# Log-sum-exp over eight heads: two heads transposed on TensorE and summed by matmuls with exp(bias), in place of three heads biased in PSUM

## The chip, the cores and the metric

The kernel runs on one core of one Trainium2 chip. The metric is the device time of one execution in microseconds (us), as the median of several runs. The core has five engines with an instruction stream each: TensorE (PE in the profile), VectorE (DVE), ScalarE (ACT), GpSimd (POOL) and SyncE (SP); here SP issues nearly all of the transfers between device memory and the on-chip SBUF. PSUM is the memory that TensorE writes.

## The reference

```python
B, S, D, H = 8, 2048, 2048, 8          # x: (B, S, D) float32, bias: (H, D // H) float32
Dh = D // H                            # 256
x_heads = x.reshape(B, S, H, Dh).transpose(0, 2, 1, 3) + bias[None, :, None, :]
x_tiled = np.repeat(x_heads, 2, axis=2)
mx = x_tiled.max(axis=-1, keepdims=True)
lse = mx.squeeze(-1) + np.log(np.exp(x_tiled - mx).sum(axis=-1))     # (B, H, 2 * S)
```

For each batch, row and head the kernel needs the logarithm of a sum of 256 exponentials of x + bias, and it writes each result twice. The input x has 134.2 MB and is read once. Both kernels compute the sum without subtracting the maximum, note in a flag whether a sum or a bias lay outside bounds within which that is safe, and branch at the end to a general routine if one did. With this input the routine is not entered.

## The kernel before, in words

**Tiles.** A tile is 256 rows of one batch: 128 partitions, K = 2 rows in each, 2048 columns, 2 MB. There are T = 64 tiles, eight to a batch. SBUF has room for eight (`xts`, which are halves of four 4 MB buffers `xbs`). Up to tile 41 one transfer brings two tiles (4 MB, L175); from `BLOCKS = 42` on one transfer brings one tile (2 MB, L187), and from tile 57 on one row of 1 MB, the last in pieces of columns. A transfer into a buffer waits until the last readers of the tiles that were in it (`last_uses`) are done. It is issued from `reload`, behind the tile after.

**A bulk tile** (tiles 0 to 53, mode `BULK`). The eight heads go three ways:
- Heads 0 to 2: TensorE puts the bias into PSUM with a matmul of a matrix of ones (L289), and adds x with an identity matmul (`late_heads`, L348). ScalarE takes exp of head 0 from PSUM and adds it up itself (L359), one instruction for each of the two rows; of heads 1 and 2 it writes the exp back over x (L366).
- Head 3: ScalarE takes exp of x without the bias, and VectorE multiplies it by exp(bias), which lies in PSUM (`later`, L416).
- Heads 4 to 7: GpSimd adds the bias to x (L398), and ScalarE takes exp (L404, together with head 3).
- VectorE then sums heads 1 to 7 of both rows in one reduction of 3584 elements in each partition (L423).

**The last tiles** have other modes: from tile 54 `MIXED`, from tile 57 row by row. There VectorE weighs a head and sums it in one instruction (`weigh`, L439) followed by one that reads the sum out; GpSimd folds one or two heads (`fold`, L455 and L463); and `keep_warm` issues three matmuls of the identity for each row (L339).

**At the end of a batch**, two tiles late, `finish` does this: VectorE clips the 128 sums of each partition, compares them and adds the result to `bad` (L482, L485, L489); TensorE transposes the sums (L496); and ScalarE takes the logarithm and doubles it (L506). `store` writes seven batches at once (L510), `finish_last` the eighth (L529).

**Order.** The order on each engine is that of the calls (a manual schedule). The two lists `for_pool` and `for_pe` put off some calls until the next tile. Waits between engines follow from the data; a reader that is known to come later than another is declared free of a wait (`on_x`).

Of the kernel before, what the change touches and what calls it, by code (L numbers as in the profile page):

```python
# [10 lines left out]
BF16 = mybir.dt.bfloat16  # L11
ACT = mybir.ActivationFunctionType
ALU = mybir.AluOpType

# [4 lines left out]
BLOCKS = 42  # L19

NBUF = 8

NEARLY = 5

NWARM = 3
# [7 lines left out]
GENERAL_B = 2  # L33

BULK = dict(pe=3, acc=1, g0=4, late=True, fold=0)
MIXED = dict(pe=1, acc=1, g0=4, late=False, fold=0)
PROMPT_F1 = dict(pe=2, acc=2, g0=8, late=False, fold=1)
PROMPT_F2 = dict(pe=2, acc=2, g0=8, late=False, fold=2)
SINGLE_F1 = dict(pe=1, acc=1, g0=8, late=False, fold=1)
TRIPLE = dict(pe=3, acc=3, g0=8, late=False, fold=0)
FOLD = 32

STAGES = [
    (0, (BULK,)),  # L50
    (54, (MIXED,)),
    (57, (PROMPT_F1, PROMPT_F1)),
    (62, (SINGLE_F1, SINGLE_F1)),
    (63, (PROMPT_F2, TRIPLE)),
]

LAST_COLS = [
    [(0, 512), (1280, 2048), (512, 1280)],
    [(0, 512), (768, 1280), (1280, 1792), (512, 768), (1792, 2048)],
]  # L60
# [3 lines left out]
def kernel(  # L64
# [11 lines left out]
    NBLK = S // (P * K)  # L76
    NB = S // (P * KB)
    TB = KB // K
    T = B * NBLK
    T_PROMPT = STAGES[1][0]  # L80
    T_FACTORS = T // 2
    CPE = BULK["pe"] * Dh
    MM = 512


    V0, W0, G0, W1, W2 = Dh, 3 * Dh, 4 * Dh, 6 * Dh, 7 * Dh
# [5 lines left out]

    brow = sb.tile([1, D], F32, name="brow")
    b_rep = sb.tile([P, D - G0], F32, name="b_rep")
    w_sb = sb.tile([P, D - W1], F32, name="w_sb")
    ident = sb.tile([P, P], F32, name="ident")
    ones = sb.tile([1, P], F32, name="ones")
    ones3 = sb.tile([3, P], BF16, name="ones3")
    b3 = sb.tile([3, CPE], BF16, name="b3")
    bparts = sb.tile([1, 3, CPE], BF16, name="bparts")  # L100
    brest = sb.tile([1, 2, CPE], F32, name="brest")
    b_flat = sb.tile([P, D // P], F32, name="b_flat")
    held = sb.tile([P, P], F32, name="held")
    out_of = sb.tile([P, P], F32, name="out_of")
    bad = sb.tile([P, P], F32, name="bad")
    ones_k = sb.tile([P, 1], F32, name="ones_k")
    flag = sb.tile([1, 1], F32, name="flag")
    g_max = sb.tile([P, GB * H], F32, name="g_max")
    g_sum = sb.tile([P, GB * H], F32, name="g_sum")
    g_res = sb.tile([P, GB, H, 2], F32, name="g_res")  # L110

    R = [sb.tile([P, KB, H, NB], F32, name=f"R{b}") for b in range(B - 1)]
    R_last = sb.tile([P, H, NBLK, K], F32, name="R_last")
    res = sb.tile([H * NB, B - 1, P, KB, 2], F32, name="res")
    res_last = sb.tile([P, P, 2], F32, name="res_last")
    xbs = [sb.tile([P, KB, D], F32, name=f"xb{i}") for i in range(NBUF // TB)]
    xts = [xb[:, k : k + K] for xb in xbs for k in range(0, KB, K)]
    w_ps = pp.tile([P, W2 - W0], F32, name="w_ps")


    one_ps = pp.tile([P, MM], F32, name="one_ps")
    pairs = [pp.tile([P, 2 * MM], F32, name=f"pair{i}") for i in range(2)]
    ps = [p[:, c : c + MM] for p in pairs for c in (0, MM)]
    tp = pp.tile([P, KB, P], F32, name="tp")

    def modes_of(t):
        return [modes for t0, modes in STAGES if t0 <= t][-1]

    def pieces(t):

        if len(modes_of(t)) == 1:
            return [(0, K, 0, D)]
        cols = [[(0, D)]] * K if t < T - 1 else LAST_COLS
        return [(k, k + 1, c0, c1) for k in range(K) for c0, c1 in cols[k]]

    def rows_of(t, n=1):


        b, at = divmod(t, NBLK)
        if b < B - 1:  # L140
            blk, i = divmod(at, TB)
            v = x[b, blk * P * KB : (blk + 1) * P * KB, :]
            return v.rearrange("(p k) d -> p k d", k=KB)[:, i * K : (i + n) * K]
        v = x[b, at * P * K : (at + 1) * P * K, :]
        return v.rearrange("(k p) d -> p k d", k=K)

    users = [[] for _ in xbs]

    def on_x(t, ins, after):
        buf = users[t // TB % len(xbs)]
        for t_u, u in buf:
            same = u.ins.engine == ins.ins.engine
            if u not in after and (not same or t_u % NBUF == t % NBUF and t_u < t):
                tc.declare_no_dep(
                    ins.ins,
                    u.ins,
                    reason="another tile, or waited for by those it waits for",
                )  # L160
        buf.append((t, ins))
        return ins

    loads = {}

    last_uses = [[] for _ in range(T)]

    def load(t):
        if TB <= t < BLOCKS:

            if t % TB == 0:
                after = [u for i in range(TB) if t >= NBUF for u in last_uses[t + i - NBUF]]
                ins = on_x(
                    t,
                    nc.sync.dma_start(  # L175
                        out=xbs[t // TB % len(xbs)], in_=rows_of(t, TB)
                    ),
                    after,
                )
                for i in range(TB):  # L180
                    loads[t + i, 0, 0] = ins
            return
        after = last_uses[t - NBUF] if t >= NBUF else []
        for k0, k1, c0, c1 in pieces(t):
            loads[t, k0, c0] = on_x(
                t,
                nc.sync.dma_start(  # L187
                    out=xts[t % NBUF][:, k0:k1, c0:c1],
                    in_=rows_of(t)[:, k0:k1, c0:c1],
                ),  # L190
                after,
            )

    def reload(t):

        n = t + NBUF
        if n < BLOCKS:
            if n % TB == TB - 1:
                load(n - TB + 1)
        elif n < T:  # L200
            load(n)
# [3 lines left out]

# [10 lines left out]
    nc.scalar.dma_start(out=brow, in_=bias.rearrange("h j -> (h j)").unsqueeze(0))  # L216
    for t in range(NBUF):
        load(t)
    nc.scalar.dma_start(
        out=b_flat, in_=bias.rearrange("h j -> (h j)").rearrange("(p c) -> p c", p=P)  # L220
    )
    nc.vector.memset(ones, 1.0)
    nc.vector.memset(ones_k, 1.0)
    nc.vector.memset(bad, 0.0)
    nc.vector.memset(ones3, 1.0)
    make_identity(nc, ident)


    bp = brow[:, 0:CPE]
    nc.gpsimd.tensor_copy(bparts[:, 0], bp)  # L230
    nc.gpsimd.tensor_sub(brest[:, 0], bp, bparts[:, 0])
    nc.gpsimd.tensor_copy(bparts[:, 1], brest[:, 0])
    nc.gpsimd.tensor_sub(brest[:, 1], brest[:, 0], bparts[:, 1])
    nc.gpsimd.tensor_copy(bparts[:, 2], brest[:, 1])
    for i in range(3):
        nc.scalar.dma_start(out=b3[i : i + 1, :], in_=bparts[:, i])

    def spread(dst, c0, c1):  # L240
        nc.tensor.matmul(  # L241
            dst, lhsT=ones, rhs=brow[:, c0:c1], start=True, stop=True
        )

    for i, c in enumerate(range(G0, D, MM)):
        spread(ps[i], c, c + MM)
        nc.vector.tensor_copy(b_rep[:, c - G0 : c - G0 + MM], ps[i])
    w_late = w_ps[:, 0 : G0 - W0]
    spread(w_late, W0, G0)
    nc.scalar.activation(out=w_late, in_=w_late, func=ACT.Exp)  # L250

    def first_factors():
        spread(one_ps, V0, W0)
        nc.scalar.activation(out=one_ps, in_=one_ps, func=ACT.Exp)

    def other_factors():
        nc.scalar.activation(
            out=w_ps[:, G0 - W0 :], in_=b_rep[:, 0 : W2 - G0], func=ACT.Exp
        )
        nc.scalar.activation(out=w_sb, in_=b_rep[:, W1 - G0 :], func=ACT.Exp)  # L260


    n_ps = [0]


    bank_users = [[], []]

    def on_bank(i, ins):
        for j, u in bank_users[i // 2]:
            if j != i and u.ins.engine != ins.ins.engine:  # L270
                tc.declare_no_dep(ins.ins, u.ins, reason="another bank")
        bank_users[i // 2].append((i, ins))
        return ins

    def put_bias(m, k0, k1):
# [3 lines left out]
        if m["late"]:  # L279
            pair = pairs[n_ps[0] % 2]  # L280
            n_ps[0] += 1
            got = [one_ps, pair[:, 0:MM], pair[:, MM : 2 * MM]]

            parts = [(ones3, b3)]
            if n_ps[0] <= NEARLY:
                parts = [(ones3[0:1], bparts[:, i]) for i in range(3)]
            for h, p in enumerate(got):
                for i, (lhsT, b) in enumerate(parts):
                    nc.tensor.matmul(  # L289
                        p,  # L290
                        lhsT=lhsT,
                        rhs=each_row(b, h * Dh, Dh, K),
                        start=i == 0,
                        stop=False,
                    )
# [427 lines left out]
```

## Time and profile before

| | us |
|---|---|
| median of 3 runs | 347.09 (346.72 to 347.30) |
| profiled execution, its time | 347.54 |
| profiled execution, its span | 345.8 |
| busy in the span: DVE / POOL / PE / ACT | 317.2 / 287.7 / 271.0 / 263.5 |
| mean granted TensorE clock | 0.879 of full speed |

The profile is of one execution. Its span reaches from the first to the last instruction; what lies around the span is 347.54 - 345.8 = 1.7 us. Busy time counts each engine's own instructions, and engines run beside one another, so an engine's share says how full it is and not whether it sets the end. For that the profile has the chain of waits: it is followed back from the last instruction, at each step to what released it. The clock row gives the clock that the throttle granted to TensorE, in tenths of full speed. GB/s is what the 16 DMA engines moved.

### The profile page before, as it was taken

The page shows a single profiled execution, that of the slowest core. Times are in us where ns is not written, and L with a number is a line of the kernel's source. Part 1 is how long each engine was busy: PE and PEld are TensorE (multiplying, and loading weights), DVE is VectorE, ACT ScalarE, POOL GpSimd, SP SyncE. Part 2 cuts the span into 40 slices and gives each one's busy share as a digit, 9 for nine tenths or more (in the row PEclk, how much of TensorE's full clock was granted, in tenths as well). Part 3 has the DMA queues.
Part 4 walks back from the last instruction along what each step waited for, and adds up shares of the span by engine and source line. Part 5 has one row for each costly group of instructions (what it writes and reads, how often), then busy time and mean ns, then how long its engine had stood idle before and what let it go on. Part 6 is the DMA issues. An engine that isn't in the chain of part 4 may idle for free.

```text
span 345.8 us, 2458 instructions
## 1 busy us (share of the span) xinstructions
PE 271.0 (78%) x695; PEld 103.0 (30%) x695; DVE 317.2 (92%) x334; ACT 263.5 (76%) x426; POOL 287.7 (83%) x120
## 2 busy tenths in 40 slices
PE   5999999697959897699758999799931989129981
PEld 2333333232313332233212333333300333005540
DVE  2256899999999999999999999999999999999995
ACT  1176699887868998599497899799930899929990
POOL 7949998999998999999989999999989993036880
PEclk9987899997987999699868899899975799858997
DMA  8999999999999999999999999999999979999500
GB/s 307 454 436 436 428 427 425 425 447 432 440 432 424 428 428 432 436 441 428 436 424 432 432 421 432 432 430 385 412 375 432 430 279 415 390 427 394 168 1 18
DMA packets 8978, 135.46 MB, mean 392 GB/s; under 512 B 1185, under 2 KB 1569, under 8 KB 2561
## 3 DMA queue, kind: packets, MB, share of 16 engines
q1 hardware_dynamic: 8720, 135.27, 92.6%
q8 instruction: 5, 0.08, 0.1%
q14 instruction: 11, 0.09, 0.1%
q10 hardware_dynamic: 242, 0.02, 0.1%
HBM read 134.23 MB, written 1.05 MB: 391 GB/s over the span
## 4 chain that ended last, share of the span: by engine, by line
DVE 78%; PE 15%; ACT 4%; issue 1%; DMA 1%
DVE R L423 52%; DVE xb L439 9%; DVE xb L416 8%; PE pair L348 6%; DVE held L482 4%; DVE bad L489 3%; PE one_ps L348 3%; PE pair L289 3%; ACT xb L404 3%; DVE out_of L485 2%; PE one_ps L289 2%; PE pair L241 1%; DVE R_last L423 1%; ACT xb L366 1%; DMA brow<-in_bias_dram 1%
## 5 line engine op out<-in xcount | busy, mean ns | idle before, releaser
L398 POOL TENSOR_TENSOR xb<-xb,b_rep 128x2048 f32<-128x2048 f32 x57 | 257.6, 4539 | 22.2 <-DMA xb<-in_x_dram 22.2
L423 DVE TENSOR_REDUCE R<-xb 128x14 f32<-128x3584 f32 (+1 forms) x56 | 214.5, 3830 | 1.9
L404 ACT ACTIVATE xb<-xb 128x2560 f32<-128x2560 f32 (+5 forms) x77 | 158.2, 2066 | 2.6 <-POOL xb L398 2.6
L348 PE MATMUL pair<-xb,ident 128*128 128x512 f32 x216 | 117.2, 671 | 0.0
L366 ACT ACTIVATE xb<-pair 128x1024 f32<-128x1024 f32 x54 | 56.9, 1054 | 18.8 <-PE pair L348 18.7
L348 PE MATMUL one_ps<-xb,ident 128*128 128x512 f32 x108 | 67.6, 711 | 3.6 <-DMA xb<-in_x_dram 3.6
L348 PEld LDWEIGHTS pair<-xb,ident 128*128 128x128 f32 x216 | 47.1, 218 | 62.6 <-issue 62.6
L416 DVE TENSOR_TENSOR xb<-xb,w_ps 128x512 f32<-128x512 f32 x54 | 36.7, 679 | 13.0 <-ACT xb L404 13.0
L359 ACT ACTIVATE xb<-one_ps 128x256 f32<-128x256 f32 x108 | 41.2, 402 | 5.8 <-PE one_ps L348 5.7
L289 PEld LDWEIGHTS <-ones 3*128 3x128 bf16 (+1 forms) x192 | 17.2, 95 | 78.0 <-issue 68.8
L289 PE MATMUL one_ps<-b,ones 3*128 3x512 bf16 x49 | 18.7, 382 | 21.3 <-ACT xb L359 21.3
L496 PE MATMUL tp<-ident,R 128*32 128x128 f32 x28 | 6.7, 335 | 35.4 <-DVE R L423 35.4
L506 ACT ACTIVATE res<-tp 32x1024 f32<-32x1024 f32 x7 | 7.1, 1012 | 33.5 <-PE tp L496 33.5
L289 PE MATMUL pair<-b,ones 3*128 3x512 bf16 x98 | 29.4, 379 | 0.0
L455 POOL TENSOR_TENSOR xb<-xb,w_sb 128x256 f32<-128x256 f32 (+1 forms) x13 | 10.0, 772 | 21.9 <-ACT xb L404 21.3
L348 PEld LDWEIGHTS one_ps<-xb,ident 128*128 128x128 f32 x108 | 17.4, 203 | 25.4 <-issue 19.1
L359 ACT ACTIVATION_READ_ACCUMULATOR xb<-one_ps 128x1 f32 x108 | 24.8, 230 | 0.0
L439 DVE CUSTOM_DVE_ANT_0 xb<-xb,w_ps 128x256 f32<-128x256 f32 x61 | 22.3, 413 | 0.0
L324 PE MATMUL pair<-xb,ident 128*128 128x512 f32 (+1 forms) x36 | 18.4, 595 | 0.0
L463 POOL TENSOR_TENSOR xb<-xb 128x128 f32<-128x128 f32 (+3 forms) x39 | 13.8, 355 | 3.1
L482 DVE TENSOR_SCALAR held<-R 128x128 f32<-128x128 f32 x7 | 14.8, 2117 | 0.0
L496 PEld LDWEIGHTS tp<-ident,R 128*32 128x32 f32 x28 | 1.8, 101 | 40.3 <-DVE R L423 38.2
(56 smaller groups left out, 136.3 us busy)
## 6 DMA issues: line engine op xcount, KB each, us to landing
xb<-in_x_dram SPq DMA_DIRECT2D x20, 4096.0 KB, 16.2
xb<-in_x_dram SPq DMA_DIRECT2D x17, 2048.0 KB, 11.7
xb<-in_x_dram SPq DMA_DIRECT2D x12, 1024.0 KB, 7.7
xb<-in_x_dram SPq DMA_DIRECT2D x4, 256.0 KB, 10.7
out_dram<-res SPq DMA_DIRECT2D x1, 896.0 KB, 6.5
xb<-in_x_dram SPq DMA_DIRECT2D x2, 384.0 KB, 10.1
xb<-in_x_dram SPq DMA_DIRECT2D x2, 128.0 KB, 6.7
out_dram<-res_last SPq DMA_DIRECT2D x1, 128.0 KB, 1.7
```

The source lines that it names most:

```text
L289: nc.tensor.matmul(p, lhsT=lhsT, rhs=each_row(b, h * Dh, Dh, K), start=i == 0, stop=False,)
L324: mm = nc.tensor.matmul(p, lhsT=ident, rhs=xts[t % NBUF][:, ka:kb, c : c + w], start=False, stop=True,)
L348: mm = nc.tensor.matmul(p, lhsT=ident, rhs=xts[t % NBUF][:, :, h * Dh : (h + 1) * Dh], start=False, stop=True,)
L359: act = nc.scalar.activation(out=xts[t % NBUF][:, k, 0:Dh], in_=got[0][:, k * Dh : (k + 1) * Dh], func=ACT.Exp, accum_out=sums[:, k, 0:1],)
L366: act = nc.scalar.activation(out=xts[t % NBUF][:, :, Dh : m["pe"] * Dh].rearrange("p k (h j) -> p h k j", j=Dh), in_=got[-1].rearrange("p ...
L398: add = nc.gpsimd.tensor_tensor(out=v, in0=v, in1=each_row(b_rep, c - G0, D - c, k1 - k0), op=ALU.add)
L404: return on_x(t, nc.scalar.activation(out=v, in_=v, func=ACT.Exp), [after])
L416: mul = nc.vector.tensor_tensor(out=f, in0=f, in1=each_row(w_ps, m["pe"] * Dh - W0, n, k1 - k0), op=ALU.mult,)
L423: red = nc.vector.tensor_reduce(out=sums[:, k0:k1, h0:H], in_=v.rearrange("p k (h j) -> p k h j", j=Dh), op=ALU.add, axis=mybir.AxisListTy ...
L439: ttr = nc.vector.tensor_tensor_reduce(out=v, in0=v, in1=w, scale=1.0, scalar=0.0, op0=ALU.mult, op1=ALU.add, accum_out=dst,)
L463: done = nc.gpsimd.tensor_tensor(out=v[:, :, 0:n], in0=v[:, :, 0:n], in1=v[:, :, n : 2 * n], op=ALU.add)
L482: nc.vector.tensor_scalar(out=c, in0=v, scalar1=lo, scalar2=hi, op0=ALU.max, op1=ALU.min)
```

## The change

The kernel is written anew around the same tiles, buffers and schedule by calls. What stays: K = 2, four buffers of 4 MB, SP as the issuer, results put off by a tile, the general routine behind a flag. What changes:

- **Heads 0 and 1** (`TH = 2`) are transposed by TensorE: eight transposes of 128x128 for a tile (`turn`), into one of two PSUM tiles `xt`. ScalarE takes exp of the 1024 columns from PSUM into SBUF (`et`). TensorE multiplies that by columns of exp(bias) (`w_cols`: 32 columns, one of them not zero) and so weighs and sums in one, into `acc` in PSUM (`weigh_turned`, four matmuls of 256 columns).
- **Heads 2 to 4**: ScalarE takes exp of x, and VectorE weighs and sums each head of each row in one instruction and its read-out (`weigh`, six for a tile), with exp(bias) in PSUM.
- **Heads 5 to 7** (`GH = 5`): GpSimd adds the bias, ScalarE takes exp, VectorE sums (`sum_biased`, 1536 elements in each partition).
- Gone: the bias by matmul, x added by identity matmuls, ScalarE's own sums, folding on GpSimd, and `keep_warm`.
- **Row by row** only from tile 58 (`WHOLE`), with no work on GpSimd: VectorE weighs heads 2 to 7 of each row.
- **Loads** of 4 MB up to tile 55 (`BLOCKS = 56`), of 2 MB up to tile 61, of 1 MB and less after; the first tile comes in two loads of 1 MB.
- **End of a batch**: the sums of heads 2 to 7 (`R`) are added to `acc` by four matmuls with the identity (`join`), ScalarE takes the logarithm from `acc`, and VectorE reduces `acc` to a sum and a minimum in each partition (`look_at`), of which the bounds are compared once, near the end.

The core of the diff:

```diff
-BLOCKS = 42
-NBUF = 8
+NBUF = 4
+WHOLE = 58
+BLOCKS = 56
+TH = 2
+GH = 5
...
-def late_heads(m, t, got, sums):
-def later(m, t, k0, k1, sums, add):
-def fold(t, k, h0, h1, sums, after):
-def keep_warm():
-def check_sums(r):
...
+    def turn(t, k0, k1, dst, h0, h1):
+        for h in range(h0, h1):
+            for c in range(CH):
+                for k in range(k0, k1):
+                    mm = nc.tensor.transpose(
+                        out=dst[:, at * P : (at + 1) * P],
+                        in_=v[:, k, col : col + P],
+                        identity=ident,
+                    )
...
+    def weigh_turned(t, k0, k1, src, h0, h1):
+        dst = acc[b % 2][:, (i * K + k0) * P : (i * K + k1) * P]
+        for c in range(h0 * CH, h1 * CH):
+            nc.tensor.matmul(
+                dst,
+                lhsT=w_cols[:, c, NB - 1 - n : NB - 1 - n + Q],
+                rhs=src[:, c * m : (c + 1) * m],
+                start=b not in started,
...
+    def finish(b):
+        for k in range(KB):
+            join(b, k)
+        log_of(b, 0, KB)
+        look_at(b, 0, KB, b)
...
+    def whole(t):
+        added = add_bias(t)
+        turn(t, 0, K, xt[i], 0, TH)
+        done = exp_of(t, 0, K, X0, XG, load_of(t, 0, K, X0, XG))
+        nc.scalar.activation(out=et[i], in_=xt[i], func=ACT.Exp)
+        run(late)
+        for k in range(K):
+            for h in range(TH, GH):
+                weigh(t, k, h, done)
+        def rest():
+            weigh_turned(t, 0, K, et[i], 0, TH)
+            biased = exp_of(t, 0, K, XG, D, [added])
+            to_release(t, sum_biased(t, biased))
+        late.append(rest)
+    def row(t, k):
...
+            if h0 < t1:
+                turn(t, k, k + 1, xt[i], h0, t1)
+            run(late)
+            if d0 < h1:
+                done = exp_of(
+                    t, k, k + 1, d0 * Dh, c1, load_of(t, k, k + 1, d0 * Dh, c1)
+                )
+            if h0 < t1:
+                nc.scalar.activation(out=et[i][:, w], in_=xt[i][:, w], func=ACT.Exp)
+            for h in range(d0, h1):
+                weigh(t, k, h, done)
```

In steady state the instructions of one tile t then stand so on each engine: on TensorE the transposes of t, then the weighing of t - 1; on ScalarE exp of heads 2 to 4 of t, exp of the transposed heads of t, then exp of heads 5 to 7 of t - 1; on VectorE the sum of heads 5 to 7 of t - 1, then the six weighings of t; on GpSimd the bias of t. `to_release` issues the next 4 MB load behind the sum of a block's second tile.

## The prediction

> **What bounds the kernel now.** First the page: busy times, the slices of clock and traffic, the chain of waits, the costliest groups.
>
> ```profile
> PE 271.0 (78%) x695; PEld 103.0 (30%) x695; DVE 317.2 (92%) x334; ACT 263.5 (76%) x426; POOL 287.7 (83%) x120
> DMA  8999999999999999999999999999999979999500
> GB/s 307 454 436 436 428 427 425 425 447 432 440 432 424 428 428 432 436 441 428 436 424 432 432 421 432 432 430 385 412 375 432 430 279 415 390 427 394 168 1 18
> DVE 78%; PE 15%; ACT 4%; issue 1%; DMA 1%
> L398 POOL TENSOR_TENSOR xb<-xb,b_rep 128x2048 f32<-128x2048 f32 x57 | 257.6, 4539 | 22.2 <-DMA xb<-in_x_dram 22.2
> L423 DVE TENSOR_REDUCE R<-xb 128x14 f32<-128x3584 f32 (+1 forms) x56 | 214.5, 3830 | 1.9
> L482 DVE TENSOR_SCALAR held<-R 128x128 f32<-128x128 f32 x7 | 14.8, 2117 | 0.0
> ```
>
> VectorE carries 78% of the chain, and yet the DMA engines are full until slice 26. So there are two limits close together. I split the span where the traffic starts to dip, and at the last landing of x:
>
> ```profile
> 10.00:240.00 230.00, 197.85 (x469) 72.09 (x468) 214.21 (x102) 186.39 (x283) 211.11 (x48) 0.90 1.00 432
> 240.00:320.00 80.00, 49.74 (x141) 19.47 (x140) 79.45 (x99) 57.72 (x97) 54.55 (x31) 0.81 0.96 391
> 324.00:345.80 21.80, 12.92 (x63) 7.05 (x61) 17.74 (x107) 13.78 (x37) 10.93 (x24) 0.88 0.03 10
> ```
>
> The last two columns are DMA share and GB/s. For 230 us the loads run at 432 GB/s, share 1.00. After 240 they fall to 391, and the last 22 us have no loads, only VectorE's backlog. Who held the loads back, from SP's waits between 240 and 320:
>
> ```profile
> SPq L187 <- DVE R L423: 71.5, 14, 14.3
> ```
>
> VectorE's reductions released the buffers late. Its price: a bulk tile costs 3.89 (L423) + 0.61 start to start (L416), 4.51 us; a batch adds the three bound instructions, (14.8 + 6.5 + 10.6) / 7 = 4.56. Eight tiles take 40.6, 5.08 a tile. A tile's load takes 2.097 MB / 0.432 = 4.85. VectorE loses 0.23 on each tile, until the eight buffers' slack is used up. So there is a floor of loads, and above it about 10 us of held loads (323.1 against 313 below) and 22 us of tail.
>
> **VectorE after the change.** Weighing a head is in the trace of the last tiles:
>
> ```profile
> L439 DVE CUSTOM_DVE_ANT_0 xb<-xb,w_ps x61: 407/414/419, 301.9 to 340.0; 128x256 f32<-128x256 f32 x61
> L439 DVE DVE_READ_ACCUMULATOR2_ANT R<- x12: 80/80/82, 301.6 to 307.5; 128x1 f32 x12
> ```
>
> Back to back they start every 0.34 us (301.57, 301.91, 302.25), also while GpSimd works. Six: 2.05. The reduction falls from 3584 to 1536 elements: 3.89 x 1536 / 3584 = 1.67. Together 3.72. The three bound instructions go; two reductions of 512 elements come, by L423 0.56 to 0.65 each, 1.2 a batch or 0.15 a tile. Sum 3.87 against 5.08. If weighing did not overlap at all (0.41 + 0.08 each) it would be 4.77, still under 4.85. The new wait is for the join: behind it on VectorE stand the sum and six weighings of the next tile, and behind those SP's next load. The wait is short unless TensorE lags.
>
> **ScalarE.** By page groups 1.48 (1536 elements), 1.05 (1024 from PSUM) and 1.48, plus 1.0 a batch: 4.1 a tile where it was 2.36 + 1.05 + 2 x 0.63 = 4.7. Hidden under 4.85. The exp of the transposed heads newly waits for eight transposes; the exp that the next sum needs is queued behind it, at most 1.7 us, beside 0.7 us of slack a tile and 14 in the buffers (below). **GpSimd:** 4.54 x 1536 / 2048 = 3.4 a tile, hidden; its cover would be gone only above 4.85.
>
> **The loads.** Two landed tiles are now released by the sum of the second, which stands behind the next block's first exp, so a block's time (9.7), three exps (4.0) and the sum (1.7) after landing: 15.4. The blocks queued behind last until 3 x 9.7 = 29.1, so nearly 14 us remain. This is why 4 MB loads up to tile 55 cost nothing so long as compute keeps under 4.85. Fewer, larger issues on SP save nothing (0.33 us each, SP idle). The store of seven batches stands behind the loads on SP and in the trace landed after them; I leave it there.
>
> **TensorE** is where the cost is open. Rates from the timeline; the first three lines are at the full clock, the last two at half:
>
> ```profile
> 157.05 1.88 PE L348 MATMUL pair<-xb,ident 128*128 128x512 f32 x4
> 319.14 0.94 PE L339 MATMUL tp<-ident 128*128 128x128 f32 x6
> 184.90 0.61 PE L496 MATMUL tp<-ident,R 128*32 128x128 f32 x4
> 312.64 1.30 PE L339 MATMUL tp<-ident 128*128 128x128 f32 x6
> 305.62 0.61 PE L496 MATMUL tp<-ident,R 128*32 128x128 f32 x2 [9.57 <-DVE R L423]
> ```
>
> A float32 matmul is two instructions, a transpose one (28 of L496 for 28 calls). Four passes of 512 columns take 1.88, the last alone 0.59: 0.43 a pass, so 0.21 for 256 columns. Transposes: (0.61 - 0.27) / 3 = 0.11. Full clock, a tile: 8 x 0.11 + 8 x 0.21 + joins 8 x 0.11 / 8 = 2.7. Half clock: 256 columns 0.43; a transpose lies between 0.19 (0.61 - 0.42, L496, with narrow weights) and 0.21 (the identity matmuls once they stream). That makes 5.1 to 5.3, above the load's 4.85. At the full clock TensorE is hidden with 2 us to spare, at half it is the bound. The before kernel ran at 0.879. I take the full side, because these windows (the first four lines filtered to L348, the last to L289) show what raised the clock:
>
> ```profile
> 16.48:19.89 3.41, 1.44 (x4) 0.49 (x3) 1.00 0.98 423
> 19.89:23.30 3.41, 3.41 (x5) 1.01 (x3) 0.50 0.91 394
> 23.30:26.72 3.42, 1.45 (x4) 0.57 (x4) 1.00 0.98 422
> 40.38:81.33 40.95, 26.54 (x57) 9.71 (x55) 1.00 0.99 428
> 16.48:19.89 3.41, 2.11 (x9) 0.76 (x9) 1.00 0.98 423
> ```
>
> The third figure from the end is the clock. A half-clock window filled by matmuls of 128 rows is followed by a full one (19.89, then 23.30 at 1.00), so a TensorE that becomes the bound fills its windows and speeds up. But the window at 16.48 was full too, 2.11 us of it matmuls of one row, and was followed by half clock: narrow work did not count. The new matmuls have 128 rows but 32 columns; no row shows how those count.
>
> A rule speaks against the change here. The Trainium skill ("TensorE: Matmul & The Clock Gate", Part 4, PE-mode transpose) says that transposes do not count as busy for the clock gate. No row of this trace shows transposes alone. By the rule the new matmuls alone would hold the clock, and the sum would lean to the first rival's 348 instead of 323.
>
> **The sum**, against the profiled execution (347.54, 0.13% above the median):
> - Loads begin to flow at 2.4 us (3.29 MB in the first 10 us at 432). 134.22 MB / 0.432 = 310.7: last landing 313.1; the 4 MB in rows at 424 add 0.2: 313.3 (before 323.1).
> - Compute starts near 16 (the bias for the bound test lands at about 10.9, then two spreads of 2.05 and an exp of 1.05), 4 us behind the loads, and gains 0.7 us a tile: no lag is left by tile 8.
> - Tail: transposes of one row 0.7, exp of 512 columns 0.6, eight passes 0.9 + 0.3, join 0.5, then what stood in before from its last logarithm on (341.57 to 345.8) 4.2: 7.3, and 9 at half clock. I take 8 (before 22.6).
> - 313.3 + 8 + 1.7 around the span = **323 us**. The rate's two halves (430 from 10 to 120, 434 from 120 to 230) give 1.5 us either way, the tail 1, partly cold TensorE some more above: own range 318 to 330.
>
> **Rivals.**
> 1. *TensorE stays at half clock and sets the pace.* Start 16, 58 tiles x 5.1, 12 rows x (4 x 0.19 + 8 x 0.21 = 2.45), 5 of tail, 1.7: 348; with 0.21 a transpose and 5.3 a tile 361; with a clock between, less, down to the forecast. It decides once 2.7 divided by the mean granted clock exceeds 4.85, at 0.56; below about 0.53 the kernel is slower than before. For: narrow work did not count, and two thirds of the new TensorE time has 32 columns. Against: full windows of 128 rows brought the clock back, and its own lag would fill them. 31%: 19 slower, 2 equal, 10 faster.
> 2. *The dip after 240 is the memory's, not VectorE's.* Then the last landing stays at 323.1, and only the tail is saved: 323.1 + 8 + 1.7 = 333. For: the share stays at 0.96 while the rate falls. Against: SP's 71.5 us of waits on VectorE. 11%, faster.
>
> **How the numbers follow.** Forecast 58%, rivals 31 and 11. Faster 0.58 + 0.10 + 0.11 = 0.79, same 0.02, slower 0.19; same means within 0.2%, about what a measurement of this kernel can tell. The range runs from the forecast's low end, 318, to rival 1's middle, 348: about 0.15 lies above it, 0.04 below.
>
> **What would show it.** Right: 430 to 434 GB/s without a dip until about 313, DVE near 255 us busy, the chain carried by DMA, SP's waits on VectorE short against the loads in flight, a tail of about 8 us. Each step has its mark: weighing at 0.34 start to start, GpSimd 3.4 an add, transposes 0.11 apart, a mean clock over 0.6. Wrong: a clock near 0.5 with PE busy at every slice and ScalarE waiting on the transposed heads (rival 1), or a dip with no wait on an engine (rival 2); or a wait for the join that holds VectorE for microseconds.

## The result, and the profile after

| | before | after |
|---|---|---|
| median | 347.19 us (346.72 to 348.08) | 343.91 us (343.86 to 343.98) |
| ratio, 95% interval | | 0.990 (0.988 to 0.992) |
| profiled execution: time, span | 347.54, 345.8 | 343.98, 342.2 |
| last landing of x (all 16 parts of the load) | 323.1 | 320.9 |
| from there to the end of the span | 22.6 | 21.3 |

The kernel became faster, by 1% and not by the 7% that was forecast: 3.3 us of 24.5. Of the missing 21.0 us (323.0 against the profiled 343.98), the last landing holds 320.9 - 313.3 = 7.6, and the tail 21.3 - 8 = 13.3.

The page of the kernel after, first the lines that answer to those of before. In the lines of the three groups (the last three): busy time and mean ns of one, then the idle time before them and its cause.

```profile
PE 248.8 (73%) x1151; PEld 141.6 (41%) x1151; DVE 256.3 (75%) x929; ACT 252.7 (74%) x215; POOL 200.7 (59%) x73
PEclk9978969888889696988888889879698888989855
DMA  7999999999999999999999999999999999999100
GB/s 314 442 456 430 431 429 433 429 431 423 429 433 429 427 433 426 429 427 430 429 430 431 441 433 433 430 423 434 433 433 439 434 400 427 425 419 404 46 2 19
DMA 67%; DVE 15%; ACT 9%; PE 6%; issue 1%; SPq 1%; ACTq 0%
L311 POOL TENSOR_TENSOR xb<-xb,b_rep 128x1536 f32<-128x1536 f32 x58 | 199.4, 3461 | 93.0 <-DMA xb<-in_x_dram 93.0
L318 DVE TENSOR_REDUCE R<-xb 128x6 f32<-128x1536 f32 x58 | 101.7, 1753 | 62.5 <-ACT xb L292 62.2
L297 DVE CUSTOM_DVE_ANT_0 xb<-xb,w_ps 128x256 f32<-128x256 f32 x396 | 140.1, 414 | 5.4 <-ACT xb L292 5.4
```

The bound has moved as forecast. VectorE fell from 317.2 to 256.3 us busy, the deep dip of the last ten slices is gone, and the chain is carried by the loads (67%) where it was carried by VectorE (78%). GpSimd waits only for data. But the last two slices of PEclk are 5, and the traffic stops three slices before the end: the tail is still there. The windows of both stretches say the same (the third column from the end is the clock):

```profile
16.00:320.00 304.00, 226.43 (x1079) 129.08 (x1077) 242.41 (x857) 240.28 (x199) 193.04 (x57) 0.85 0.99 425
320.00:342.00 22.00, 10.73 (x46) 6.55 (x46) 10.10 (x55) 5.43 (x9) 0.00 (x0) 0.54 0.04 11
```

No engine is busy for even half of those last 22 us. What they consist of stands in the chain in order of time (start, us, what):

```profile
323.39 0.41 DVE seen L349 x2
323.94 1.88 PE acc L275 x8
325.82 0.44 PE acc L326 x2
326.29 0.40 ACT res_last L344
326.71 0.49 DVE seen L349 x2
327.33 1.88 PE acc L275 x8
329.21 0.44 PE acc L326 x2
```

This is a ring: the weighing of one row (L275) into `acc`, its join (L326), its logarithm (L344), the bounds read out of `acc` (L349), and only then the weighing of the next row. One turn takes 327.33 - 323.94 = 3.4 us, while six weighings, VectorE's work on a row, take 2.05. The waits stand in the timeline of the same stretch:

```profile
321.48 0.38 PE L326 MATMUL acc<-ident,R 128*32 128x128 f32 x2 [3.90 <-DVE R L297]
321.89 0.40 ACT L344 ACTIVATE res_last<-acc 32x256 f32<-32x256 f32 x1 [4.01 <-PE acc L326]
327.33 1.88 PE L275 MATMUL acc<-et,w_cols 128*32 128x128 f32 x8 [1.08 <-DVE seen L349]
```

The first two lines are one wait passed on. The join of the first of the last four rows waited 3.90 us for VectorE's weighings; ScalarE stood in its queue at the logarithm, 4.01 us, with the exp of the next row behind it. The eight passes of L275 then take 1.88, against the 1.06 that the same group took at 308.07.

### The profile page after: what moved, and what is told of

Read it like the earlier page. It is cut to its first block, busy times and chain, and to the rows that moved or that the text cites. A ratio compares the mean times of both kernels' runs of the same rounds, so it can differ in the third digit from the quotient of the medians.

```text
span 342.2 us, 3767 instructions
## 1 busy us (share of the span) xinstructions
PE 248.8 (73%) x1151; PEld 141.6 (41%) x1151; DVE 256.3 (75%) x929; ACT 252.7 (74%) x215; POOL 200.7 (59%) x73
## 4 chain that ended last, share of the span: by engine, by line
DMA 67%; DVE 15%; ACT 9%; PE 6%; issue 1%; SPq 1%; ACTq 0%
DMA xb<-in_x_dram 67%; DVE xb L297 8%; DVE R L318 6%; ACT xb L292 5%; PE xt L258 4%; ACT et L453 3%; PE acc L275 2%; DVE seen L349 1%; SPq L160 1%; PE acc L326 0%; ACT res_last L344 0%; PE xt L381 0%; DVE R L297 0%; ACT et L484 0%; DVE row_clip L231 0%
## 5 line engine op out<-in xcount | busy, mean ns | idle before, releaser
L311 POOL TENSOR_TENSOR xb<-xb,b_rep 128x1536 f32<-128x1536 f32 x58 | 199.4, 3461 | 93.0 <-DMA xb<-in_x_dram 93.0
L292 ACT ACTIVATE xb<-xb 128x1536 f32<-128x1536 f32 x129 | 186.2, 1467 | 44.7 <-DMA xb<-in_x_dram 44.7
L275 PE MATMUL acc<-et,w_cols 128*32 128x256 f32 (+1 forms) x560 | 152.9, 427 | 4.7 <-ACT et L484 2.5
L318 DVE TENSOR_REDUCE R<-xb 128x6 f32<-128x1536 f32 x58 | 101.7, 1753 | 62.5 <-ACT xb L292 62.2
L297 DVE CUSTOM_DVE_ANT_0 xb<-xb,w_ps 128x256 f32<-128x256 f32 x396 | 140.1, 414 | 5.4 <-ACT xb L292 5.4
L258 PE MATMUL xt<-ident,xb 128*128 128x128 f32 x512 | 87.0, 321 | 74.0 <-DMA xb<-in_x_dram 74.0
L258 PEld LDWEIGHTS xt<-ident,xb 128*128 128x128 f32 x512 | 66.8, 163 | 106.2 <-DMA xb<-in_x_dram 86.3
L275 PEld LDWEIGHTS acc<-et,w_cols 128*32 128x32 f32 x560 | 64.9, 127 | 72.7 <-issue 36.0
L453 ACT ACTIVATE et<-xt 128x1024 f32<-128x1024 f32 x58 | 59.0, 1018 | 16.1 <-PE xt L258 15.7
L297 DVE DVE_READ_ACCUMULATOR2_ANT R<- 128x1 f32 x420 | 33.6, 80 | 0.0
L326 PE MATMUL acc<-ident,R 128*32 128x128 f32 x64 | 9.7, 287 | 3.9 <-DVE R L297 3.9
L349 DVE TENSOR_REDUCE seen<-acc 32x1 f32<-32x512 f32 (+1 forms) x20 | 10.3, 552 | 2.4 <-ACT res_last L344 2.4
L326 PEld LDWEIGHTS acc<-ident,R 128*32 128x32 f32 x64 | 7.2, 116 | 6.2 <-issue 4.1
L344 ACT ACTIVATE res_last<-acc 32x256 f32<-32x256 f32 x4 | 1.6, 393 | 10.9 <-PE acc L326 10.9
L297 DVE CUSTOM_DVE_ANT_0 xb<-xb,w_sb 128x256 f32<-128x256 f32 x24 | 9.0, 407 | 0.0
L344 ACT ACTIVATE res<-acc 32x1024 f32<-32x1024 f32 x7 | 7.0, 1004 | 0.8 <-PE acc L326 0.8
```

The lines of the kernel that those rows point to most:

```text
L258: mm = nc.tensor.transpose(out=dst[:, at * P : (at + 1) * P], in_=v[:, k, col : col + P], identity=ident,)
L275: nc.tensor.matmul(dst, lhsT=w_cols[:, c, NB - 1 - n : NB - 1 - n + Q], rhs=src[:, c * m : (c + 1) * m], start=b not in started, stop=b == ...
L292: ins = nc.scalar.activation(out=v, in_=v, func=ACT.Exp)
L297: ins = nc.vector.tensor_tensor_reduce(out=v, in0=v, in1=weights(h), scale=1.0, scalar=0.0, op0=ALU.mult, op1=ALU.add, accum_out=sums_of(t ...
L311: ins = nc.gpsimd.tensor_tensor(out=v, in0=v, in1=repeated(b_rep, 0, D - XG, K), op=ALU.add)
L318: ins = nc.vector.tensor_reduce(out=sums_of(t, 0, K, GH, H), in_=v, op=ALU.add, axis=AXIS.X)
```

## The experiments

Three questions: what holds the tail (the ring of the last rows, the half clock, the 4 MB loads that release two tiles at once, or simply VectorE's own rows), why the loads end 7.6 us late, and what the last 3 us behind VectorE's flag are. Each time stands against runs of the kernel before on the same chip (medians 346.85 to 347.9). These medians differ by 1 us between the groups of runs, so a difference between experiments of different groups is no finer than that where only times are compared.

**1. Loads of 2 MB from tile 42 on, as before the change.**

```diff
-BLOCKS = 56
+BLOCKS = 42
```

> Loads of 2 MB from tile 42 on (4 MB to tile 55 in the changed kernel); nothing else. Theory A (4 MB landings keep VectorE idle and then leave it about 9 us behind the loads at the last block, and it works that off in the tail): VectorE follows each tile, the first of the last four rows is weighed near 316 us and not at 321, the last transposes start near 325 and not at 331, time 337 to 340. Theory B (the tail is long because TensorE is at half clock there, 0.54): the tail keeps its 21 us after the last landing, time 343 to 344. The last landing stays at 320 to 321 by both, one DMA engine still 4 to 5 us behind the others.

Measured: 342.60 us (342.05 to 343.54), 0.988 (0.985 to 0.991) of before, 1.3 under the kernel after. The last part of x landed at 321.5, as late as ever, and the tail still took 19.3. Theory A missed: VectorE came to the first bounds (L349) of the ring at 321.96 where the kernel after has 323.32, 1.4 us earlier and not 5. So the 4 MB loads are a small part of the tail and no part of the late landing.

**2. The last four rows finished together.** `row` no longer finishes the row before it; at the end all four are joined, one logarithm is taken of 1024 columns, the result is stored, and only then are the bounds read.

```diff
-                finish_row(at_end)
...
-    finish_row(KB - 1)
+    for k in range(KB):
+        join(B - 1, k)
+    log_of(B - 1, 0, KB)
     store_last()
+    for k in range(KB - 1):
+        look_at(B - 1, k, k + 1, B - 1 + k)
+    count_early()
     count_last()
```

> The last four rows are finished together behind the last row (four joins, one logarithm, then the bounds), not each behind the next row. Theory A2 (in the tail each row's matmuls into acc wait for the reads of the row before: 3.4 us a row in a chain through TensorE, ScalarE and VectorE): the chain goes, VectorE ends near 326 and not 332, time 337 to 339. Theory B (half clock): only the 0.9 us that each row's eight passes lose at half clock could be saved, and they stay; time 343 to 344.

Measured: 338.59 us (338.08 to 340.18), 0.977 (0.974 to 0.981) of before, 5.3 under the kernel after: a hit. The timeline of this kernel's tail:

```profile
322.86 1.06 PE L275 MATMUL acc<-et,w_cols 128*32 128x128 f32 x8 [0.75 <-ACT et L483]
327.68 1.01 ACT L344 ACTIVATE res_last<-acc 32x1024 f32<-32x1024 f32 x1 [4.88 <-PE acc L326]
328.73 1.27 DVE L349 TENSOR_REDUCE seen<-acc 32x1 f32<-32x128 f32 x6 [1.77 <-ACT res_last L344]
```

The weighing of a row no longer waits for L349 and runs at the full clock. What the ring cost came from the order of the calls: the joins and bounds are still all there, and one logarithm of 1024 columns stands for four of 256.

**3. Full clock in the tail, with the ring left in.** In front of the first of the four late joins, where TensorE idles, stand 16 matmuls of the identity.

```diff
+            if at_end == 0:
+                for _ in range(16):
+                    nc.tensor.matmul(acc[0][:, 0:P], lhsT=ident[:, 0:Q],
+                                     rhs=ident, start=True, stop=True)
```

> On the changed kernel as it is: 16 identity matmuls into the free accumulator (no one reads them) in front of the first of the four late joins, where TensorE waits 3.9 us for VectorE. Theory B (half clock in the tail costs): TensorE stays at full clock, each row's eight passes take 0.95 and not 1.9, the chain falls from 3.4 to about 2.3 us a row, time 339 to 341. If the waits alone make the chain (VectorE's weighing, 2.05 a row, close behind), 342.5 to 344.

Measured: 340.53 us (340.25 to 342.98), 0.984 (0.980 to 0.989) of before, 3.4 under the kernel after, within theory B's range. The timeline of the added work and of a row's weighing, and the window of the tail:

```profile
317.44 3.66 PE L489 MATMUL acc<-ident 128*32 128x128 f32 x32
324.07 1.03 PE L275 MATMUL acc<-et,w_cols 128*32 128x128 f32 x8 [1.50 <-DVE seen L349]
326.52 1.03 PE L275 MATMUL acc<-et,w_cols 128*32 128x128 f32 x8 [1.20 <-ACT xb L292]
```

```profile
320.00:340.00 20.00, 7.30 (x57) 5.08 (x54) 10.15 (x57) 5.43 (x9) 0.00 (x0) 0.88 0.04 12
```

3.66 us of matmuls that compute nothing held the clock at 0.88 where it was 0.54. A turn of the ring fell from 3.4 to 2.45 us. These 3.4 us overlap with the 5.3 of experiment 2, where the weighing runs at the full clock too (1.06). What the half clock would cost without the ring, no run shows. The added matmuls have 128 rows and 32 columns, and TensorE did nothing else in these 3.66 us: so such work keeps the clock up.

**4. Experiments 1 and 2 in one kernel.**

> Both edits: 2 MB from tile 42, last four rows finished together. If the two losses are separate, VectorE ends near 323 and the time is 333 to 335; if they are the same backlog seen twice, no better than the better of the two alone, 337 to 339. Theory B: 342 to 344.

Measured: 337.43 us (337.19 to 337.55), 0.972 (0.970 to 0.974) of before: 1.2 under experiment 2. The time lies in the range of "the same backlog seen twice", but for another reason: the two gains add up (1.3 + 5.3 = 6.6, here 6.5), so the losses are separate, and the one from the loads is smaller than the forecast had it. The chain in order of time shows what is left. VectorE's weighings (L297) are left out here, as are some other instructions; between the second line and the third VectorE works without a gap:

```profile
261.35 29.63 DMA xb<-in_x_dram
...
294.81 1.75 DVE R L318
...
326.20 0.42 PE acc L326 x2
326.64 1.02 ACT res_last L344
327.69 1.28 DVE seen L349 x6
```

VectorE has twelve rows of six weighings left when tile 57 is in: 12 x 6 x 0.343 = 24.7 us. It starts on tile 57 only once that load has landed in full (the first line ends at 291.0), and then runs behind the loads to the end, 4.7 us past the last landing at 321.5. In this state the landing of tile 57 moves everything behind it. The last landing does not: in experiment 7 it came 1.2 us later (322.7), and VectorE wrote the flag at the same time (330.53, here 330.54).

**5. Why the loads end late.** Each load has 16 parts, one on each DMA engine. In the trace's landings, one part falls further and further behind the others:

| kernel after: load complete at, us | 22.7 | 43.4 | 82.5 | 132.0 | 181.5 | 231.0 | 280.6 | 320.9 |
|---|---|---|---|---|---|---|---|---|
| last part behind the first, us | 0.4 | 1.7 | 1.9 | 2.9 | 3.8 | 4.8 | 5.8 | 6.5 |
| last part behind the 15th, us | 0.2 | 0.8 | 0.2 | 1.1 | 2.0 | 3.0 | 4.0 | 4.9 |

The other fifteen spread over at most 1.8 us (at 82.5 three parts are late together, so the second row is small there). From 129 us on the distance grows in steps of about 1 us, and at each step lies a packet of 8 KB on the queue for instructions: at 129.3, 178.9, 222.3, 273.1 and 311.0 us, with two more before them at 32.7 and 81.0. By the trace's records VectorE ran 120 to 133 instructions from each of these seven packets to the next; it has some 2.7 for each microsecond now, 929 in all where it had 334.

Up to the last landing there are twelve other packets for instructions: four of 8 KB (82.7, 155.5, 231.5, 313.7), 62 to 84 ScalarE instructions apart, and eight of 16 KB on a second queue (the first at 37.8, the last at 295.1). From 129 us on none of these alone makes a step of the last part; behind each of 16 KB one more of the other parts is about 1.6 us late. So VectorE's packets seem to meet the same DMA engine each time; the trace does not name the engine. In the kernel before, the distance behind the 15th stayed below 1.7 and was made up again when VectorE held the loads back.

The theory was that each fetch of instructions delays one of the 16 engines by about 1 us, and that a queue which is never idle never gives it back. First doubling: 13 one-element memsets on VectorE in each whole tile.

```diff
+        for _ in range(13):
+            nc.vector.memset(idle, 0.0)
```

> Each of the 58 whole tiles gets 13 more instructions on VectorE, memsets of one element that no one reads (about 0.06 us each, 0.8 us a tile, which VectorE's idle time can hide in the middle). Theory C (one DMA engine falls behind because VectorE's instructions are fetched over it, about 1 us for each 8 KB of 128 instructions): fetches twice as often, the lag of that engine at the end near 9 us instead of 4.9, last landing near 325, time 348 to 352. Rival (the lag belongs to the deeper queue of 4 MB loads): lag stays at 5 us, time 343 to 347, the dummies of the last tiles adding up to 3 us to VectorE's backlog.

Measured: 364.50 us (364.3 to 364.81), 1.050 (1.048 to 1.053) of before. The time can't be read as meant, as the timeline of one tile shows (from one sum, L319, to the next):

```profile
153.79 1.73 DVE L319 TENSOR_REDUCE R<-xb 128x6 f32<-128x1536 f32 x1
157.51 1.32 DVE L460 MEMSET idle<- 1x1 f32 x12
158.88 1.75 DVE L319 TENSOR_REDUCE R<-xb 128x6 f32<-128x1536 f32 x1
```

The memsets start 0.11 us apart (12 in 1.32), not the 0.06 counted on. VectorE's tile became 158.88 - 153.79 = 5.1 us, above the load's 4.85, and VectorE became the bound. But before that bit, the distance did what the theory says: 5.0 us behind the 15th part at 184.6 (6.6 behind the first), with seven fetches of VectorE's up to there (24.3 to 183.3, here 118 to 140 instructions apart), where the kernel after has 2.0 (3.8) at 181.5 with four. That is about 0.95 us for each fetch in both. Once VectorE held the loads back, the distance behind the 15th shrank to 1.0 (at 275.7) and then grew again to 3.0.

**6. The fetches halved and more.** The kernel of experiment 4, without the weighing of heads 2 to 4 in the whole tiles.

```diff
         for k in range(K):
-            for h in range(TH, GH):
-                weigh(t, k, h, done)
```

> On the kernel of both edits (2 MB from tile 42, rows finished together, 337.4 us); left out: VectorE's weighing and summing of heads 2 to 4 in the 58 whole tiles (their sums are set to 1). VectorE goes from 13 to 1 instruction a tile. Theory C (the lag of one DMA engine comes from fetching VectorE's instructions): lag at the end at most 2 us instead of 5.0, last landing 317 to 318.5 instead of 321.5, time 331 to 334. Rival (the lag belongs to the deep queue or to that engine): lag stays near 5, last landing 321 to 322; then only VectorE's backlog goes, 334 to 336.

Measured: 330.79 us (330.04 to 332.22), 0.955 (0.952 to 0.958) of before. The page, with the instruction count of VectorE in the last figure of its item:

```profile
PE 235.1 (72%) x1151; PEld 134.3 (41%) x1151; DVE 138.8 (42%) x233; ACT 251.8 (77%) x212; POOL 201.2 (61%) x81
```

233 instructions on VectorE, and the last load of x was complete less than 0.1 us behind its fifteenth part: at 316.6, where experiment 4 had 321.5. That is the 4.9 us. Two things went away together here, the instructions and VectorE's use of SBUF. For the instructions speak the steps at the packets, and experiment 5, whose memsets hardly use SBUF: there the distance grew with the number of fetches. VectorE's branch at the end was short too (below), which is part of the 6.6 us between this kernel and experiment 4.

**7. The last 3 us.** In the kernel after, VectorE takes its branch on the flag and then needs 3.1 us to its next instruction (338.24 to 341.33 in the trace's records; experiment 4: 331.67 to 334.90); before the change it was 0.56 (343.64 to 344.20). The theory: whether the code behind the branch has been fetched by then depends on where the branch lies in VectorE's instruction stream. So the stream is shifted by 64 one-element memsets at about 10 us, where VectorE has nothing else to do, on the kernel of experiment 4:

```diff
+    for _ in range(64):
+        nc.vector.memset(idle, 0.0)
```

> On the kernel of both edits: 64 memsets of one element more on VectorE while it waits for the first exp (near 10 us), nothing else. Theory F (of the 4.8 us behind the last instruction 2 to 3 are VectorE's branch past the general routine waiting for instructions to be fetched, which depends on where in the stream the branch stands): the gap between VectorE's branch and its end falls from 3.2 us to under 1, time 334.5 to 336. Rival (the end has this length by itself): 337 to 338. The lag of the DMA engine stays near 5 us.

Measured: 335.16 us (335.05 to 335.9), 0.967 (0.965 to 0.969) of before. The timeline's last instruction on VectorE's way to the flag is as in experiment 4, where it stood at 330.54:

```profile
330.53 0.28 DVE L397 TENSOR_REDUCE flag<-xt 1x1 f32<-1x128 f32 x1 [0.48 <-PE xt L384]
```

The branch is followed by the next instruction after 0.58 us (331.66 to 332.24). All of the gain, 2.3 us, lies behind the flag, though this kernel executes 64 instructions more. The distance of the last part behind the 15th did not stay near 5: it was 6.1, with one more fetch ahead of the last landing.

Half the shift, to see how fine the place is:

```diff
-    for _ in range(64):
+    for _ in range(32):
```

> On the same kernel: 32 memsets in place of 64, nothing else. If the place of VectorE's instructions against the 8 KB fetches decides, the branch at the end stays short (under 1 us) or is long again (about 3), and one fetch fewer falls before the last load: lag 5.1 or 6.1. Time 334 to 335 with a short branch, 337 with a long one. If the place does not matter, 335 as with 64.

Measured: 335.20 us (335.11 to 335.54), 0.964 (0.960 to 0.967) of before; the branch took 0.58 us again. So 32 instructions are enough. Counted in the records, the branch stands behind 935 VectorE instructions in the kernel after and in experiment 4, behind 967 and 999 with the memsets, and behind 1021 in the last kernel below, where it took 2.96 us again: it is the place and not the number that decides. That the branch waits for the fetch of its code fits all of these cases, but was not seen as such: in the long cases three packets of 8 KB for instructions lie within the wait (339.2 to 340.2 in the kernel after), in the short ones they come behind it, and the trace does not say which of them is VectorE's.

**8. Fewer rows, and more.** Row by row from tile 62 in the kernel of experiment 4, and from tile 56 in that of experiment 7.

```diff
-WHOLE = 58
+WHOLE = 62
```

> On the kernel of both edits: row by row only from tile 62, not 58, so VectorE has 3.7 us of work a tile for four more tiles in place of 4.1. If VectorE's work after tile 57 sets the tail (it is busy without a gap from 295 to 326), 1.5 us less work: 335 to 336.5. If the wait for each next tile's exp matters more (a whole tile's last sum is put off by a tile), no gain or slower, 337 to 339.

Measured: 339.19 us (339.03 to 339.81), 0.978 (0.976 to 0.980) of before, 1.8 slower than experiment 4. VectorE's waits for ScalarE's third exp at the put-off sum grew (total, times, longest; from 280 us on), here from 62 on:

```profile
DVE R L318 <- ACT xb L292: 8.0, 7, 1.4
```

and here from 58 on:

```profile
DVE R L318 <- ACT xb L292: 4.4, 4, 1.5
```

```diff
-WHOLE = 58
+WHOLE = 56
```

> On the kernel with 2 MB from tile 42, rows finished together and 64 memsets (335.2 us): row by row from tile 56, not 58. Row by row from 62 was slower by 1.8, which spoke for the put-off last sum of a whole tile as the cost. If so, two tiles more in rows leave VectorE nearer to the loads at tile 58 and gain 0.5 to 1: 334.2 to 334.7. If VectorE's work (4.1 us a tile in rows, 3.7 in whole tiles) matters as much, 335 to 336.

Measured: 336.81 us (336.69 to 338.09), 0.971 (0.969 to 0.973) of before, 1.65 slower than experiment 7. By the time alone this is a miss. The timeline shows where the time went:

```profile
329.97 0.28 DVE L397 TENSOR_REDUCE flag<-xt 1x1 f32<-1x128 f32 x1 [0.47 <-PE xt L384]
```

VectorE is no later at the flag than in experiment 7 (330.53) but 0.56 us earlier. What makes this kernel slower lies behind the flag: with 22 VectorE instructions more ahead of it the branch takes 2.96 us (331.10 to 334.06) instead of 0.58. With the short branch it would come to 334.4 by these numbers (336.81 less 2.4), which is in the forecast's first range; that is an estimate, and no run tested it. So 58 is better than 62. Between 56 and 58 the times decide nothing but the branch: the 0.56 us are from one profile of each kernel, and the runs of one kernel spread by more. For rows from tile 54 there is no time.

The best version that was timed is that of experiment 7: 335.16 us, 11.7 under the kernel before in the same runs, and 8.8 under the kernel after.

## Why the prediction was right and wrong

**Right: what bounds, and the prices of the steps.** The direction was called, by the mechanism that was named: VectorE's busy time fell to 256.3 us where about 255 was forecast, the loads had no deep dip, and the chain was carried by DMA. The weighing started every 0.34 us (323.72, 324.06, 324.40 in the trace), the sum took 1.75 where 1.67 was scaled, GpSimd's add 3.46 against 3.4, eight transposes 1.10 us (155.79), the eight passes of 256 columns 1.91 (156.82) against 8 x 0.21 = 1.7.

**Rival 1 (half clock all along) did not come**: the mean clock over the bulk was 0.85. TensorE's timeline alternates: at 151.46 eight transposes took 1.97, at 155.79 in the same burst 1.10. A burst of two tiles warms itself and cools in the wait for the next load (TensorE was idle for 3.91 us ahead of 151.46). So the new work does count; that matmuls of 128 rows and 32 columns alone hold the clock, the point that was open, experiment 3 shows. Against the Trainium skill ("TensorE: Matmul & The Clock Gate", Part 4, PE-mode transpose) this decides nothing, since no run shows transposes alone; the lean towards 348 that was drawn from it was not borne out. Where the half clock did come is the tail, which the forecast had only as 9 us in place of 7.3: after TensorE's idle 3.9 us (317.6 to 321.5) the clock was 0.54 to the end. The same page (Part 1) has the clock fall after about one idle window of 3.4 us; the row agrees.

**Rival 2 (the dip belongs to the memory) is refuted**: with VectorE out of the way the rate stays at 433 to 439 from slice 28 to 32, where it had gone down to 375.

**Wrong 1: "last landing 313.3".** It was 320.9. The step "134.22 MB / 0.432" took the mean rate as if all 16 engines ended together. Fifteen had ended by 316.0 (2.7 late: the mean was 431 over 10 to 240 and 424 from there to 316), the sixteenth 4.9 later. The change itself made this term: it nearly tripled VectorE's instructions (334 to 929), and the fetches of instructions travel on the same DMA engines. The forecast had counted those instructions only by their time on VectorE. How much of the time this lag is worth was not measured alone: by the chain of experiment 4 what counts is how late it makes tile 57 (4.0 us behind the 15th part then), not the last landing.

**Wrong 2: "Tail: ... 7.3, and 9 at half clock. I take 8".** It was 21.3. The terms add up to 7.2, but that is not the fault: the sum followed one row from its landing to the end. Four things were not in it, sized by the runs (they overlap in part):

| in the tail, not priced | us | from |
|---|---|---|
| ring of the last four rows: weigh, join, logarithm, bounds (3.4 with the half clock alone put right) | 5.3 | experiments 2, 3 |
| branch that waits behind the flag | 2.3 | experiment 7 |
| 4 MB loads up to tile 55 | 1.2 to 1.3 | experiments 1, 4 |
| VectorE's own row backlog: 4.7 us of weighings between the last landing and the last join, where 0.7 + 0.6 + 0.9 + 0.3 = 2.5 were reckoned | about 2 | chain of experiment 4 |

These make 11 of the 13.3 us. With the first three taken out (32 memsets, experiment 7) the end comes 333.4 - 321.4 = 12.0 us behind the last landing; of the 4 us that this is still above the forecast, about 2 are VectorE's backlog and some 2 were not assigned. The first is the worst of them as a step: the new edges of `acc`, from L349 to the next L275, stand in the diff, and the text said of a wait only that it might be "for the join that holds VectorE". Here VectorE held the join, and the join ScalarE. And "4 MB loads up to tile 55 cost nothing" was right for the bulk and wrong by 1.2 to 1.3 us for the end; by which step, was not shown.

**The range** held the time (318 to 348), but only because of rival 1's end. Its upper part stood for another mechanism, so that it held was luck. The forecast's own range ended at 330.

## What to carry to other kernels

When a change takes the bound away from an engine and leaves it with the loads, price the last tile anew: follow every accumulator from its writer to its last reader and back to the next writer, and count what runs as a ring there. A load queue that was never idle did not regain here what it had lost, so many small instructions were paid twice, on the engine and as fetches on the DMA engines. Put the reads that nobody waits for (here the bounds) behind those that someone waits for. And compare two versions at their last piece of work too, not only at the end: a branch behind it moved the end by 2.4 us and hid what the change itself did.

## What the hardware showed that was not expected

- One of the 16 parts of each load fell behind by about 0.95 us for each 8 KB fetch of VectorE's instructions (four fetches 3.8 us in the kernel after, seven 6.6 in experiment 5). At the end it was 4.9 us behind the 15th; with 233 instead of 929 instructions on VectorE less than 0.1.
- A branch past the general routine cost VectorE 0.56 to 0.58 or 2.8 to 3.2 us, by where it lay in the instruction stream: long behind 935 instructions, short behind 967 and 999, long behind 1021.
- Memsets of one element start 0.11 us apart on VectorE.
- 3.7 us of matmuls in an idle stretch (128 rows, 32 columns) kept the tail's clock at 0.88 instead of 0.54.
